# A hybrid decoder layer on one core: the router's logits summed by a picking product, membership written as bf16, and the expert weights and the first splits placed elsewhere

## The chip, the cores and the metric

One Trainium2 chip, one core. The metric is the device time of one execution in microseconds (us); the median of three runs stands for a kernel. Engines in the tables: PE is TensorE, PEld its weight loads, DVE VectorE, ACT ScalarE, POOL GpSimd, SP SyncE (here it issues nearly all DMAs).

## The reference

A layer for 512 tokens of 2048 channels. A mixer (causal pooling and a gated DeltaNet side by side) is added to the residual h; then comes the part that the change touches, a mixture of experts with two-level routing; then a gated per-layer embedding and a final norm.

```python
logits_grp = xf @ w_rg + b_rg                    # 4 groups
gi = argmax(logits_grp); p_sel = softmax(logits_grp)[gi]
logits_exp = (xf @ w_re + b_re).reshape(t, 4, 8)
le = logits_exp[gi]                              # the 8 experts of the chosen group
top_vals, top_idx = lax.top_k(le, 2)
weights = p_sel[:, None] * softmax(top_vals)
...                                              # tokens sorted by expert, in blocks
hmid = silu(xb @ w_gate[e]) * (xb @ w_up[e])     # 2048 -> 512
acc[idx] += (hmid @ w_down[e]) * wt[:, None]     # 512 -> 2048
```

`xf` is rms_norm(h). 32 experts of 12 MB each are read once.

## The kernel before

Tokens lie on partitions in NT = 4 tiles of 128 (P = 128, T = 512, KD = 16 blocks of 128 channels).

`project_out` makes h column block by column block. For each block of 128 channels it transposes h (`h_transposed`), copies the result to `hT` and multiplies with the router's 36 columns `wr` (4 groups and 32 experts). Even blocks add up in partitions 0 to 35 of the PSUM bank `pl`, odd ones in partitions 64 to 99, so the logits are there in two halves, with tokens along the free axis. The last of these products (L921) is followed by the router.

`router` first computes rstd on DVE. Then `L` (named lgT in the rows), which GpSimd had set to zero, takes the two halves of `pl` by two ACT copies (L945); four PE transposes (L947) turn it so that tokens lie on partitions; an ACT copy (L949) brings the bank to SBUF as `l2`; DVE adds the two halves (L960), multiplies by rstd (L961) and adds the bias (L962). `first_max` (L967 to L973) picks the best group (`og`) and then, twice, the best expert (`o1`, `o2`) with tiny DVE operations, each of which reads what the one before wrote. The membership M (L988) is copied to bf16 as `Mb` (L992); ten small products with `Mb` (L995) count the tokens in front, and `rank` (L998) is the place of each token with its expert. The rest of `router` makes the weights of the two chosen experts (`dg`, `gth`, `den`, `psel`, `dm`, `td`, `w`, `wj`, and `aux` in the end), with two tanh on ACT in it.

`spots` makes the 0/1 matrices `G` from `rank` (L1131): eight of 128x128 for the first two units, one per unit and token tile, then larger ones. `gather` multiplies h with `G` (L1161, L1162) to collect the tokens of a unit, 16 channel blocks, two at a time. Each channel block of h, read with a stride of four elements, is first split into a high part `ghi` (ACT, L96) and a low part `glo` (DVE, L97), two buffers each; `L` has the first `ghi` buffer and `l2` the first `glo` buffer, so they are in the same rings. The first two splits, of blocks 0 and 1, may run before the ranks are known.

After that PE multiplies with the expert weights (L1181 up, L1243 down). The weights come in 1 MB transfers through a ring of 16 tiles (`fill_stream`, L1112): SyncE issues the next transfer when PE has used up a tile, and for experts 8 to 31 it reads the expert's number from the table that `order_experts` makes during the first unit.

The order of the instructions of PE is that of the code from `experts` on; on the other engines, and in the router, a scheduler sets it. `behind(ins)` lets what stands in its body be issued only after the given instructions.

Of the kernel before, what the change touches and what calls it, by code (L numbers as in the profile page):

```python
# [9 lines left out]
F32 = mybir.dt.float32  # L10
# [4 lines left out]
OP = mybir.AluOpType  # L15
AX = mybir.AxisListType

P = 128
T = 512
NT = T // P  # L20
# [44 lines left out]
class Layer:  # L65
# [28 lines left out]

    def split(self, hi, lo, src):
        i = self.nc.scalar.copy(hi, src)  # L96
        return i, self.nc.vector.tensor_tensor(lo, src, hi.bitcast(F32), op=OP.subtract)  # L97

# [27 lines left out]
    def constants(self):  # L126
        nc, c, tmp = self.nc, self.consts, self.px
# [3 lines left out]
        nc.gpsimd.iota(pi, pattern=[[0, 1]], base=0, channel_multiplier=1)  # L131
        d = self.below
        self.upper = self.p_dc.tile([P, P], F32, name="upper", bufs=1)
        nc.vector.tensor_scalar(self.upper, d, 0.0, None, op0=OP.is_ge)
# [42 lines left out]
        pr = tmp.tile([P, 8], I32, name="c_pr", bufs=1)  # L177
# [755 lines left out]
    def router(self, pp, pm):  # L933
        nc = self.nc
        pl = self.pl
# [3 lines left out]
        rstd = pp.tile([P, NT], F32, name="rs2", bufs=1)  # L939
# [3 lines left out]
        pt = self.bank("dl")  # L943
        for o in (0, 64):
            nc.scalar.copy(L[o:o + 36, :], pl[o:o + 36, :])  # L945
        for t in range(NT):
            nc.tensor.transpose(pt[:, t * P:(t + 1) * P], L[:, t * P:(t + 1) * P], self.ident)  # L947
        l2 = pm.tile([P, NT, 2, 64], F32, name="l2", tag="glo", bufs=2)
        nc.scalar.copy(l2.rearrange("p t i c -> p (t i c)"), pt)  # L949

        def t_(name, *dims):
            return pp.tile([P, NT, *dims], F32, name=name, bufs=1)

        def bc(x, *dims):
            return x.to_broadcast([P, NT, *dims])

        tt, ts, stt = nc.vector.tensor_tensor, nc.vector.tensor_scalar, nc.vector.scalar_tensor_tensor
        red = nc.vector.tensor_reduce
        lg = t_("lg", 36)
        tt(lg, l2[:, :, 0, 0:36], l2[:, :, 1, 0:36], op=OP.add)  # L960
        tt(lg, lg, bc(rstd[:, :, None], 36), op=OP.mult)  # L961
        tt(lg, lg, bc(self.br[:, None, :], 36), op=OP.add)  # L962
# [23 lines left out]
        tt(o12, o1, o2, op=OP.add)  # L986
        M = t_("M", 4, 8)
        tt(M, bc(og[:, :, :, None], 4, 8), bc(o12[:, :, None, :], 4, 8), op=OP.mult)  # L988
        pr = self.bank("mm")
        Mf = M.rearrange("p t g j -> p t (g j)")  # L990
        Mb = self.p_rt.tile([P, NT, N_EXP], BF16, name="Mb", bufs=1)
        nc.vector.tensor_copy(Mb, Mf)  # L992
        for t in range(NT):
# [3 lines left out]
        self.rank = self.p_rt.tile([P, NT, N_EXP], F32, name="rank", bufs=1)  # L997
        stt(self.rank, pr[:, 0:128].rearrange("p (t e) -> p t e", t=NT), 1.0, Mf, op0=OP.add, op1=OP.mult)  # L998
        self.dump("rank", self.rank)
        dg = t_("dg", 4)  # L1000
        tt(dg, lg[:, :, 0:4], bc(gm, 4), op=OP.subtract)
# [24 lines left out]
        nc.vector.tensor_copy(self.aux[:, :, :, 0], bc(rstd[:, :, None], 4))  # L1026
        self.Mb = Mb

# [107 lines left out]

    def gather(self, pp, G, c0, homes):

# [5 lines left out]
        def parts(k):  # L1144
            hi = pp.tile([P, NT, P], F32R, name="ghi", bufs=2)
            lo = pp.tile([P, NT, P], F32R, name="glo", bufs=2)
            self.split(hi, lo, hs[:, :, k // 4, k % 4, :])
            return hi, lo
# [120 lines left out]
    def experts(self, pp):  # L1269
# [13 lines left out]
        def gathered(*us, spot=None, **kw):  # L1283
            if spot:
                spots(spot, *us, **kw)
            for u in us:
                xe[u] = self.p_xe.tile([P, KD, P], F32, name="xe", tag=f"xe{u % 4}", bufs=1)
            yield from self.gather(pp, *G[us[0]], [xe[u] for u in us])

# [504 lines left out]
```

## Time and profile before

| | |
|---|---|
| median of 3 runs | 2546.78 us (2546.51 to 2548.41) |
| profiled execution | 2548.15 us |
| its span in the trace | 2546.4 us |
| PE busy | 2411.1 us (95% of the span) |
| DVE busy | 1063.4 us (42%) |
| ACT busy | 719.8 us (28%) |
| POOL busy | 83.6 us (3%) |
| DMA | 554.13 MB, mean 218 GB/s |

Times in the rows count from the start of the span. Work outside the span takes 2548.15 - 2546.4 = 1.75 us of the profiled execution. A busy share over the whole span is a mean over stages with different limits: the mixer before 1336 us, the router from 1342 to 1356 us, the experts until 2340 us, the last gate and norm after that.

### The profile page before, as it was taken

To read this page: it belongs to the slowest core of one execution; us is meant where nothing else is said; L and a number is where in the kernel's file an instruction comes from. 1 tells how busy PE (TensorE), PEld (TensorE's weight loads), DVE (VectorE), ACT (ScalarE), POOL (GpSimd) and SP (SyncE) were. 2 spreads that over 40 slices of the span, in tenths; PEclk is the share of its full clock that TensorE was granted. 3 is DMA by queue.
4 is the path that set the end of the run, shared out by engine and by line. 5 is a ranking of instruction groups with operands and counts; after the bars stand their busy time and mean duration, and the time that the engine had idled before them with its cause. 6 is when DMAs were issued, how large, how long until landed. Compare 5 with 4: busy or idle time off the path is not lost. (4 is left out here: it accounts for less than half of the span.)

```text
span 2546.4 us, 30523 instructions
## 1 busy us (share of the span) xinstructions
PE 2411.1 (95%) x11926; PEld 1652.8 (65%) x11926; DVE 1063.4 (42%) x1963; ACT 719.8 (28%) x1323; POOL 83.6 (3%) x92
## 2 busy tenths in 40 slices
PE   7999999999999999999998978999989989987998
PEld 6788888888888888877774523533533433353888
DVE  6475757665422232334445412422423312324435
ACT  5233332423322222224445401400311300114323
POOL 1001011100000000000000000000000000000002
PEclk9999999999999999999998999999999999999999
DMA  5232222233233233247226799999999999998322
GB/s 158 76 88 67 76 72 81 67 97 124 91 99 99 92 99 98 93 155 275 90 88 235 290 386 421 420 421 421 420 421 421 420 380 421 419 419 304 116 83 100
DMA packets 201047, 554.13 MB, mean 218 GB/s; under 512 B 30377, under 2 KB 127042, under 8 KB 152130
## 3 DMA queue, kind: packets, MB, share of 16 engines
q1 hardware_dynamic: 197682, 543.61, 56.2%
q10 hardware_dynamic: 2640, 4.33, 0.5%
q0 software_dynamic: 576, 4.19, 0.4%
q8 instruction: 95, 1.56, 0.3%
q14 instruction: 54, 0.44, 0.0%
HBM read 545.01 MB, written 7.08 MB: 217 GB/s over the span
## 5 line engine op out<-in xcount | busy, mean ns | idle before, releaser
L1181 PE MATMUL ps_mm<-wm,xe 128*64 128x512 f32 (+1 forms) x2048 | 437.9, 607 | 46.5 <-DMA wm<-in_w_up_dram 28.6
L101 PE MATMUL ps_mm<-n1h,whi 128*128 128x512 f32 x1120 | 450.3, 402 | 0.9 <-ACT whi L96 0.9
L103 PE MATMUL ps_mm<-n1h,wlo 128*128 128x512 f32 x1120 | 437.3, 391 | 1.5 <-DVE wlo L97 1.4
L102 PE MATMUL ps_mm<-n1l,whi 128*128 128x512 f32 x1120 | 437.1, 390 | 0.0
L97 DVE TENSOR_TENSOR wlo<-raw,whi 128x1024 fp32r<-128x1024 f32 x206 | 254.5, 1235 | 408.9 <-ACT whi L96 401.1
L96 ACT CAST whi<-raw 128x1024 fp32r<-128x1024 f32 x206 | 216.3, 1050 | 545.1 <-PE ps_mm L102 544.2
L1181 PEld LDWEIGHTS ps_mm<-wm,xe 128*64 128x64 f32 (+1 forms) x2048 | 123.6, 128 | 322.7 <-issue 211.1
L1267 DVE TENSOR_TENSOR h<-h,ps_dl 128x512 f32<-128x512 f32 x208 | 130.2, 682 | 387.6 <-PE ps_dl L1265 387.6
L103 PEld LDWEIGHTS ps_mm<-n1h,wlo 128*128 128x128 f32 x1120 | 210.0, 188 | 47.2 <-DVE wlo L97 2.4
L101 PEld LDWEIGHTS ps_mm<-n1h,whi 128*128 128x128 f32 x1120 | 210.8, 188 | 40.3 <-ACT whi L96 1.3
L102 PEld LDWEIGHTS ps_mm<-n1l,whi 128*128 128x128 f32 x1120 | 210.9, 188 | 38.5
L1243 PE MATMUL ps_mm<-wm,hmT 128*64 128x512 f32 (+1 forms) x896 | 192.1, 610 | 16.7 <-DMA wm<-in_w_down_dram 7.4
L97 DVE TENSOR_TENSOR glo<-h,ghi 128x512 fp32r<-128x512 f32 x80 | 88.7, 1120 | 126.6 <-ACT ghi L96 126.2
L1243 PEld LDWEIGHTS ps_mm<-wm,hmT 128*64 128x64 f32 (+1 forms) x896 | 55.1, 131 | 123.1 <-issue 99.2
L96 ACT CAST ghi<-h 128x512 fp32r<-128x512 f32 x80 | 90.2, 1146 | 137.4 <-PE ps_dl L1161 97.4
L1161 PE MATMUL ps_dl<-G,ghi 128*128 128x384 f32 (+1 forms) x320 | 101.9, 332 | 1.0 <-DVE G L1131 1.0
L103 PE MATMUL ps_mm<-whi,ml 128*128 128x512 f32 x256 | 100.7, 393 | 2.1 <-DVE ml L97 2.1
L101 PE MATMUL ps_mm<-whi,mh 128*128 128x512 f32 x256 | 100.8, 394 | 0.0
L102 PE MATMUL ps_mm<-wlo,mh 128*128 128x512 f32 x256 | 100.7, 394 | 0.0
L1162 PE MATMUL ps_dl<-G,glo 128*128 128x384 f32 (+1 forms) x320 | 98.1, 320 | 1.0 <-DVE glo L97 1.0
L1227 ACT ACTIVATE yhi<-ps_mm,sc 128x512 fp32r<-128x512 f32 x52 | 35.7, 690 | 205.9 <-PE ps_dl L1264 113.6
L1228 DVE SCALAR_TENSOR_TENSOR ylo<-ps_mm,sc,yhi 128x512 fp32r<-128x512 f32 x52 | 39.0, 751 | 118.7 <-ACT yhi L1227 116.6
(417 smaller groups left out, 3292.3 us busy)
## 6 DMA issues: line engine op xcount, KB each, us to landing
wm<-in_w_gate_dram SPq DMA_DIRECT2D x128, 1024.0 KB, 18.9
wm<-in_w_up_dram SPq DMA_DIRECT2D x128, 1024.0 KB, 17.8
wm<-in_w_down_dram SPq DMA_DIRECT2D x128, 1024.0 KB, 19.8
raw<-in_w_in_dram SPq DMA_DIRECT2D x144, 512.0 KB, 3.5
raw<-in_w_out_dram SPq DMA_DIRECT2D x32, 512.0 KB, 3.6
wm<-in_w_ple_gate_dram SPq DMA_DIRECT2D x16, 1024.0 KB, 5.1
raw<-in_w_up_dn_dram SPq DMA_DIRECT2D x16, 512.0 KB, 3.5
raw<-in_w_up_pool_dram SPq DMA_DIRECT2D x16, 512.0 KB, 3.4
```

What stands on the lines that cost most here:

```text
L96: i = self.nc.scalar.copy(hi, src)
L97: return i, self.nc.vector.tensor_tensor(lo, src, hi.bitcast(F32), op=OP.subtract)
L101: mm(ps, whi, xhi, start=start, stop=False)
L102: mm(ps, whi, xlo, start=False, stop=False)
L103: mm(ps, wlo, xhi, start=False, stop=stop)
L1161: nc.tensor.matmul(p, hi[:, t, :], G[:, t, c0:c0 + n], start=t == 0, stop=False)
L1162: nc.tensor.matmul(p, lo[:, t, :], G[:, t, c0:c0 + n], start=False, stop=t == NT - 1)
L1181: nc.tensor.matmul(ps[w * i:w * i + w, :], xe[:, k, w * i:w * i + w], ws[i][:, j, :], start=k == 0, stop=k == KD - 1)
L1227: nc.scalar.activation(yh, ps, AF.Copy, scale=sc[:, 2:3])
L1228: nc.vector.scalar_tensor_tensor(yl, ps, sc[:, 2:3], yh.bitcast(F32), op0=OP.mult, op1=OP.subtract)
L1243: nc.tensor.matmul(out[cb][r, :], hT[:, k, r], ws[i][:, cb * T:(cb + 1) * T], start=k == 0, stop=k == 3)
L1267: nc.vector.tensor_tensor(d, d, pc, op=OP.add)
```

## The change

The router is written anew in five places, and the first two splits of `gather` change engine:

1. The second half of the logits is copied to `L` by DVE, not by ACT.
2. The four transposes become four products with `pick`, a 128x36 matrix with ones where the row is the column or the column plus 64. They transpose and add both halves at once, into 36 columns per token tile. The copy to `l2` and the addition go; the multiplication by rstd reads PSUM.
3. M and its copy become one multiplication that writes `Mb` as bf16; `rank` reads `Mb`.
4. What makes the experts' weights moves into a function `shares`, behind the membership.
5. The low parts of blocks 0 and 1 of the first gather are computed by GpSimd.

```diff
-    def split(self, hi, lo, src):
+    def split(self, hi, lo, src, eng=None):
         i = self.nc.scalar.copy(hi, src)
-        return i, self.nc.vector.tensor_tensor(lo, src, hi.bitcast(F32), op=OP.subtract)
+        return i, (eng or self.nc.vector).tensor_tensor(lo, src, hi.bitcast(F32), op=OP.subtract)
...
+        self.pick = c.tile([P, 36], F32, name="pick")
+        nc.vector.scalar_tensor_tensor(self.pick, d[:, 0:36], -64.0, self.ident[:, 0:36], op0=OP.is_equal, op1=OP.add)
...
         pt = self.bank("dl")
-        for o in (0, 64):
-            nc.scalar.copy(L[o:o + 36, :], pl[o:o + 36, :])
+        nc.scalar.copy(L[0:36, :], pl[0:36, :])
+        nc.vector.tensor_copy(L[64:100, :], pl[64:100, :])
         for t in range(NT):
-            nc.tensor.transpose(pt[:, t * P:(t + 1) * P], L[:, t * P:(t + 1) * P], self.ident)
-        l2 = pm.tile([P, NT, 2, 64], F32, name="l2", tag="glo", bufs=2)
-        nc.scalar.copy(l2.rearrange("p t i c -> p (t i c)"), pt)
+            nc.tensor.matmul(pt[:, t * 36:(t + 1) * 36], L[:, t * P:(t + 1) * P], self.pick, start=True, stop=True)
+        l = pt[:, 0:NT * 36].rearrange("p (t c) -> p t c", t=NT)
...
-        tt(lg, l2[:, :, 0, 0:36], l2[:, :, 1, 0:36], op=OP.add)
-        tt(lg, lg, bc(rstd[:, :, None], 36), op=OP.mult)
+        tt(lg, l, bc(rstd[:, :, None], 36), op=OP.mult)
         tt(lg, lg, bc(self.br[:, None, :], 36), op=OP.add)
...
-        M = t_("M", 4, 8)
-        tt(M, bc(og[:, :, :, None], 4, 8), bc(o12[:, :, None, :], 4, 8), op=OP.mult)
         pr = self.bank("mm")
-        Mf = M.rearrange("p t g j -> p t (g j)")
         Mb = self.p_rt.tile([P, NT, N_EXP], BF16, name="Mb", bufs=1)
-        nc.vector.tensor_copy(Mb, Mf)
+        member = tt(Mb.rearrange("p t (g j) -> p t g j", j=8), bc(og[:, :, :, None], 4, 8),
+                    bc(o12[:, :, None, :], 4, 8), op=OP.mult)
...
-        stt(self.rank, pr[:, 0:128].rearrange("p (t e) -> p t e", t=NT), 1.0, Mf, op0=OP.add, op1=OP.mult)
+        stt(self.rank, pr[:, 0:128].rearrange("p (t e) -> p t e", t=NT), 1.0, Mb, op0=OP.add, op1=OP.mult)
         self.dump("rank", self.rank)
+        self.Mb = Mb
+        with self.behind((member,)):
+            self.shares(t_, bc, rstd, lg, gm, og, m1, m2, o1, o2)
+
+    def shares(self, t_, bc, rstd, lg, gm, og, m1, m2, o1, o2):
...
         dg = t_("dg", 4)
         tt(dg, lg[:, :, 0:4], bc(gm, 4), op=OP.subtract)
...
-    def gather(self, pp, G, c0, homes):
+    def gather(self, pp, G, c0, homes, first=False):
...
-            self.split(hi, lo, hs[:, :, k // 4, k % 4, :])
+            self.split(hi, lo, hs[:, :, k // 4, k % 4, :], nc.gpsimd if first and k < 2 else nc.vector)
...
-            yield from self.gather(pp, *G[us[0]], [xe[u] for u in us])
+            yield from self.gather(pp, *G[us[0]], [xe[u] for u in us], first=us[0] == 0)
```

Two lines are added above the router, so that a line of before stands two to eight lines further down in the kernel after it (L945 becomes L946 and L947, L1131 becomes L1137).

VectorE at the entry of the router, before. `rs` is rstd, `aux` and `glo` are as above, `lg` are the logits, `gm` their maximum over the groups; what stands in brackets is the engine whose signal the instruction waits for.

```order
L1026 COPY aux<-rs_10308 128x16 [waits DVE_49]
L97 TENSOR_TENSOR glo<-h,ghi 128x512
L960 TENSOR_TENSOR lg<-l_10330 128x144 [waits Activation_49]
L961 TENSOR_TENSOR lg<-lg,rs_10308 128x144 [waits DVE_49]
L97 TENSOR_TENSOR glo<-h,ghi 128x512 [waits Activation_49]
L962 TENSOR_TENSOR lg<-lg,br 128x144 [waits DVE_49]
L967 TENSOR_REDUCE gm<-lg 128x4 [waits DVE_49]
```

And after the change:

```order
L89 SCALAR_TENSOR_TENSOR rs_10310<-rsq_b_10312,rsq_j_10311 128x4 [waits DVE_49]
L947 COPY lgT<-ps_dl 36x512 [waits Activation_49]
L961 TENSOR_TENSOR lg<-ps_dl,rs_10310 128x144 [waits DVE_49,PE_49]
L962 TENSOR_TENSOR lg<-lg,br 128x144 [waits DVE_49]
L967 TENSOR_REDUCE gm<-lg 128x4 [waits DVE_49]
L969 TENSOR_TENSOR ge<-lg,gm 128x16 [waits DVE_49]
```

Both splits and the addition have left this place, and the copy to lgT has come to it; it waits for a signal of ScalarE, which in the row of its queue below is its copy of the other half.

ScalarE from there on, after the change:

```order
L946 COPY lgT<-ps_dl 36x512 [waits PE_49,Pool_49]
L96 CAST ghi<-h 128x512 [waits DVE_49,PE_49]
L1010 ACTIVATE gth<-dg 128x16 [waits DVE_49]
L1021 ACTIVATE td<-dm 128x4 [waits DVE_49]
L96 CAST ghi<-h 128x512 [waits PE_49,Pool_49] x2
```

The copies to the second half and to `l2` are gone. The split that follows waits for PE, since its buffer is the one that `L` had; the two tanh (`gth`, `td`) stand behind it, as before.

GpSimd after the change, behind its zeroing of `L`:

```order
L944 MEMSET lgT 128x512 [waits DVE_49]
L1393 IOTA ei 128x32
L97 TENSOR_TENSOR glo<-h,ghi 128x512 [waits DMAHW3_49,DMAHW1_49,DMAHW6_49,DMAHW0_49,Activation_49]
L97 TENSOR_TENSOR glo<-h,ghi 128x512 [waits Activation_49]
L1356 TENSOR_LOAD n_over [waits DVE_49]
```

The two subtractions with `glo` are new in this queue; before, its MEMSET and IOTA were followed at once by the load of `n_over`.

VectorE from the membership to the matrices `G`, before:

```order
L988 TENSOR_TENSOR M<-ge,o_10366 128x128 [waits DVE_49]
L1022 TENSOR_TENSOR wj<-wj 128x4x8 [waits DVE_49]
L992 CAST Mb<-M 128x128 [waits DVE_49]
L1024 TENSOR_TENSOR aux<-ge,wj 128x16x8 [waits DVE_49]
L998 SCALAR_TENSOR_TENSOR rank<-ps_mm,M 128x128 [waits PE_49]
L1131 TENSOR_TENSOR G_10420<-slot,rank 128x128 [waits DVE_49]
L1131 TENSOR_TENSOR G_10420<-slot,rank 128x128 x7
L1131 TENSOR_TENSOR G_10903<-slot,rank 128x4x128 x2
```

And after:

```order
L989 TENSOR_TENSOR Mb<-ge,o_10365 128x128 [waits DVE_49]
L1008 TENSOR_TENSOR dg<-lg,gm 128x16
L1019 TENSOR_TENSOR dm<-am,bm 128x4
L1033 COPY aux<-rs_10310 128x16
L1012 TENSOR_SCALAR den<-gth 128x16 [waits Activation_49]
L1023 TENSOR_SCALAR w_10397<-td 128x4 [waits Activation_49]
L1024 TENSOR_SCALAR w_10397<-td 128x4
L1013 RECIPROCAL den<-den 128x16 [waits DVE_49]
L996 SCALAR_TENSOR_TENSOR rank<-ps_mm,Mb 128x128 [waits PE_49]
L1014 SCALAR_TENSOR_TENSOR den<-gth,den 128x16 [waits DVE_49]
L1137 TENSOR_TENSOR G_10417<-slot,rank 128x128 [waits DVE_49]
L1016 TENSOR_REDUCE psel<-den 128x4 [waits DVE_49]
```

The operations of the weights, which stood between those of the selection, now stand behind the membership: seven of them between `Mb` and `rank`, of which two wait for a tanh of ScalarE, and then one or two behind each of the first six `G`.

## Rows read from the trace of the kernel before

**Rows 1.** Busy time by stage, from the end of the router to the end of the expert weights. Columns: the stretch and its length in us; for each engine the busy us and the number of instructions; PEclk, the granted TensorE clock as a share of full speed; the mean busy share of the 16 DMA engines; GB/s.

```profile
1348.50:1363.00 14.50, 7.18 (x42) 6.65 (x41) 11.31 (x50) 4.80 (x9) 0.00 (x0) 0.54 0.01 4
1363.00:1400.00 37.00, 37.00 (x207) 19.26 (x208) 16.51 (x14) 22.22 (x42) 0.00 (x0) 1.00 0.82 312
...
1485.00:2340.00 855.00, 777.89 (x3861) 337.00 (x3859) 245.32 (x387) 160.27 (x303) 0.00 (x0) 0.98 1.00 414
```

**Rows 2.** What the queue on SyncE that issues the weight transfers waited for between 1330 and 1480 us. Columns: who waited, for whom, us in total, times, longest us.

```profile
SPq L1112 <- PE ps_mm L1181: 75.6, 14, 21.8
...
SPq L1049 <- DVE nb L1426: 9.3, 1, 9.3
```

**Rows 3.** Timeline of the router's entry: from the copies of the two halves of the logits to the addition of the bias. Columns: start in us, duration in us, engine, line, operation, out<-in, count, and in brackets the idle time before it with what ended it.

```profile
1344.58 1.17 ACT L945 COPY lgT<-ps_dl 36x512 f32<-36x512 f32 x2 [1.90 <-PE ps_dl L921]
1345.85 0.63 PE L947 MATMUL ps_dl<-ident,lgT 128*128 128x128 f32 x4 [1.36 <-issue]
1346.51 0.59 ACT L949 COPY l<-ps_dl 128x512 f32<-128x512 f32 x1 [0.76 <-PE ps_dl L947]
1347.00 1.10 ACT L96 CAST ghi<-h 128x512 fp32r<-128x512 f32 x1
1347.13 0.31 DVE L960 TENSOR_TENSOR lg<-l 128x144 f32<-128x144 f32 x1 [1.52 <-ACT l L949]
1347.48 0.31 DVE L961 TENSOR_TENSOR lg<-lg,rs 128x144 f32<-128x144 f32 x1
1348.13 1.06 DVE L97 TENSOR_TENSOR glo<-h,ghi 128x512 fp32r<-128x512 f32 x1 [0.35 <-ACT ghi L96]
1349.11 0.30 DVE L962 TENSOR_TENSOR lg<-lg,br 128x144 f32<-128x144 f32 x1
```

**Rows 4.** Timeline of the chain of small operations on VectorE, with those of the expert weights between them. Columns as in rows 3.

```profile
1349.74 0.17 DVE L1001 TENSOR_TENSOR dg<-lg,gm 128x16 f32<-128x16 f32 x1
1349.86 0.17 DVE L970 TENSOR_TENSOR ge<-ge,prio 128x16 f32<-128x16 f32 x1
1349.94 0.21 ACT L1003 ACTIVATE gth<-dg 128x16 f32<-128x16 f32 x1 [1.84 <-DVE dg L1001]
1350.19 0.17 DVE L1005 TENSOR_SCALAR den<-gth 128x16 f32<-128x16 f32 x1
1350.27 0.17 DVE L973 TENSOR_TENSOR ge<-ge,gq 128x16 f32<-128x16 f32 x1
1350.40 0.25 DVE L1006 RECIPROCAL den<-den 128x16 f32<-128x16 f32 x1
1350.57 0.29 DVE L978 TENSOR_TENSOR le<-lg,ge 128x128 f32<-128x128 f32 x1
...
1353.69 0.19 DVE L986 TENSOR_TENSOR o<-ae,be 128x32 f32<-128x32 f32 x1
...
1354.01 0.28 DVE L988 TENSOR_TENSOR M<-ge,o 128x128 f32<-128x128 f32 x1
...
1354.33 0.23 DVE L992 CAST Mb<-M 128x128 bf16<-128x128 f32 x1
```

**Rows 5.** Timeline from the ranks to the first gather products. Columns as in rows 3.

```profile
1354.61 0.18 PE L995 MATMUL ps_mm<-Mb,before 128*128 128x32 bf16 x1 [8.13 <-DVE Mb L992]
...
1355.07 0.29 DVE L998 SCALAR_TENSOR_TENSOR rank<-ps_mm,M 128x128 f32<-128x128 f32 x1 [0.32 <-PE ps_mm L995]
1355.40 0.90 DVE L1131 TENSOR_TENSOR G<-slot,rank 128x128 fp32r<-128x128 f32 x4
1356.04 0.55 PE L1161 MATMUL ps_dl<-G,ghi 128*128 128x256 f32 x1 [1.00 <-DVE G L1131]
...
1357.46 0.41 PE L1161 MATMUL ps_dl<-G,ghi 128*128 128x256 f32 x1
```

**Rows 6.** Prices read elsewhere. First two rows of a timeline at an expert unit (columns as in rows 3): four products of a 128x128 stationary tile with 9 columns, and four transposes. Then instructions by line: count, duration in ns as minimum/median/maximum, first and last start, shapes.

```profile
1404.55 1.06 PE L1193 MATMUL ps_dl<-aux,G 128*128 128x9 f32 x8
1405.46 0.64 PE L1195 MATMUL ps_dl<-ident,G 128*128 128x128 f32 x4
...
L917 DVE COPY hT<-ps_dl x8: 684/691/693, 1195.4 to 1342.7; 128x512 f32<-128x512 f32 x8
...
L97 DVE TENSOR_TENSOR glo<-h,ghi x80: 1057/1108/1797, 1344.6 to 1999.5; 128x512 fp32r<-128x512 f32 x80
L97 DVE TENSOR_TENSOR ml<-m,mh x64: 684/692/694, 1145.3 to 1330.9; 128x512 fp32r<-128x512 f32 x64
```

**Rows 7.** Timelines of GpSimd and of VectorE at the first chunk of the delta rule, where both work at once. Columns as in rows 3.

```profile
142.76 0.16 DVE L668 TENSOR_TENSOR s<-rk 128x4 f32<-128x4 f32 x1
142.86 1.30 POOL L687 TENSOR_TENSOR bd<-B,diag 128x512 f32<-128x512 f32 x1 [56.98 <-DVE B L684]
142.96 1.22 DVE L669 TENSOR_TENSOR s<-s,beta 128x4 f32<-128x4 f32 x1
...
148.93 1.28 POOL L713 TENSOR_TENSOR E<-E,upper 128x512 f32<-128x512 f32 x1
149.01 1.05 DVE L689 TENSOR_REDUCE bc<-bd 128x64 f32<-128x512 f32 x1 [0.80 <-POOL bd L687]
```

**Rows 8.** GpSimd's elementwise operations on 128x512: by line, with duration in ns as minimum/median/maximum, and by shape, with count | busy us, mean ns | idle before.

```profile
L636 POOL TENSOR_TENSOR gm<-upper,ghi x8: 1040/1050/1712, 81.1 to 481.0; 128x512 fp32r<-128x512 f32 x8
...
L687 POOL TENSOR_TENSOR bd<-B,diag 128x512 f32<-128x512 f32 x8 | 10.3, 1286 | 109.7 <-DVE B L684 80.5 <-DVE s L668 29.2
```

More of the change, by code (lines that the diff above doesn't have):

```diff
@@ L997, in router @@
         self.rank = self.p_rt.tile([P, NT, N_EXP], F32, name="rank", bufs=1)
-        stt(self.rank, pr[:, 0:128].rearrange("p (t e) -> p t e", t=NT), 1.0, Mf, op0=OP.add, op1=OP.mult)
+        stt(self.rank, pr[:, 0:128].rearrange("p (t e) -> p t e", t=NT), 1.0, Mb, op0=OP.add, op1=OP.mult)
         self.dump("rank", self.rank)
+        self.Mb = Mb
+        with self.behind((member,)):
+            self.shares(t_, bc, rstd, lg, gm, og, m1, m2, o1, o2)
+    def shares(self, t_, bc, rstd, lg, gm, og, m1, m2, o1, o2):
+        nc = self.nc
+        tt, ts, stt = nc.vector.tensor_tensor, nc.vector.tensor_scalar, nc.vector.scalar_tensor_tensor
+        red = nc.vector.tensor_reduce
         dg = t_("dg", 4)
@@ L1026, in router @@
         nc.vector.tensor_copy(self.aux[:, :, :, 0], bc(rstd[:, :, None], 4))
-        self.Mb = Mb
     def units(self):
```

## The prediction, made before the changed kernel was run

> **What bounds the kernel now.** I read the busy time by stage first, then the waits of the queue that issues the weights, then the timeline of the router, instruction by instruction. The reader is to see three things.
>
> First, the longest stage, 1485 to 2340 us, is bound by transfers: DMA share 1.00 at 414 GB/s, while PE works 777.89 of 855 us [rows 1]. Nothing in the router makes these 855 us shorter; it can only make them begin sooner. Second, they can begin sooner: between 1348.5 and 1363 us the DMA share is 0.01, since the ring is full, and from 1363 to 1400 PE is busy 37.00 of 37.00 us [rows 1]. The queue that issues the weights waited 75.6 us in 14 waits for PE's up products and 9.3 us for the table of experts, which is itself made behind the first unit [rows 2]. So what the router saves before the first gather product should move all that follows, nearly one for one. Third, in the router PE does nothing for 8.13 us before the rank products [rows 5]; the path runs over ACT and DVE, one small operation after the other.
>
> The path in rows: ACT begins its copies at 1344.58, DVE begins to add the halves at 1347.13 and the bias at 1349.11 [rows 3], M at 1354.01 [rows 4], rank at 1355.07, PE the first gather product at 1356.04 [rows 5]: 11.46 us.
>
> **The change part by part.** Gains are positive; all times are on that path.
>
> *Two engines copy.* DVE's copy waits for ScalarE alone, yet it needs the last router product of PE. Only ACT's copy of the other half has waited for that, so the signal must be that copy's: the two run one after the other, not side by side. Before, they end at 1344.58 + 1.17 = 1345.75 [rows 3]. After: 0.58 for ACT, 0.03 from engine to engine (PE's end 1346.48 to ACT's 1346.51 [rows 3]), and 0.69 for DVE by its copies of 512 elements from PSUM [rows 6]: 1345.88. **-0.13**; were they side by side, 1345.27 and +0.48.
>
> *Picking products.* A transpose is one pass, a product of f32 with f32 two: four transposes show 4 instructions, four products 8, with 0.64 against 1.06 us [rows 6]. **-0.42.** Nine columns there, 36 here; bounds 0 (no dearer) and -0.8 (twice that difference). PE begins 0.10 behind the copies as before, at 1345.98, and ends at 1345.98 + 0.63 + 0.42 = 1347.03.
>
> *The copy to `l2` and the addition.* From PE's end at 1346.48 to DVE at 1347.13 there are 0.65 us [rows 3]; one passage of 0.03 stays: **+0.62**. The addition takes 1347.48 - 1347.13: **+0.35**. Reading PSUM instead costs nothing visible: rank, from PSUM, takes 0.29 [rows 5], M, from SBUF, 0.28 [rows 4].
>
> *The second split leaves DVE.* It sits between the multiplication by rstd and the bias: 1349.11 - 1347.48 = 1.63 us, where the step before took 0.35 [rows 3]: **+1.28**. The first split fills a wait of DVE before 1347.13; moving it gains nothing.
>
> *The weights leave the chain.* Most hide in the gaps between dependent operations: with `dg` and `den` among them the two steps from L970 to L973 take 1350.27 - 1349.86 = 0.41. Only where a reciprocal stands between (1350.57 - 1350.27 = 0.30) and ahead of M, where two `wj` do (1354.01 - 1353.69 = 0.32), is it more than some 0.21 [rows 4]: **+0.19**.
>
> *Where the second split goes.* On GpSimd it meets DVE's chain. Rows show what follows: while POOL ran 142.86 to 144.16, a DVE operation on 128x4 with two SBUF inputs took 1.22 us instead of 0.16 and ended 0.02 behind POOL; a reduction beside the next POOL operation kept its 1.05 [rows 7]. After the change, the multiplication by rstd starts at 1347.03 + 0.03 = 1347.06, the bias at 1347.41. ACT may split `ghi` of block 1 only when the products have released `L`, so 1347.06 to 1348.16 (1.10 [rows 3]); POOL begins then, or behind L970, which starts 0.75 after the bias [rows 4] at 1348.16 and ends at 1348.33. L973, with two SBUF inputs, is due 1.16 after the bias, at 1348.57, and L978 at 1348.77 (1.46, less the reciprocal's 0.10). If POOL takes d, L973 ends 0.02 after 1348.33 + d and L978 starts 0.03 later. For d, contiguous operations show 1.05 and 1.29 [rows 8]; but h is read with stride four, which takes DVE from 0.692 to 1.108 us [rows 6], 1.60 times. I take 1.05 x 1.60 = 1.68, nearest in kind: L978 starts at 1350.06. **-1.29**; with d = 1.05 it is -0.66, with no lock 0.
>
> The Trainium skill (GPSIMD Engine Reference, section 4.1, Engine selection) holds an elementwise operation with two inputs on GpSimd to be about 2 times slower than on VectorE and advises against it. This trace has 1.05 against 0.692, 1.5 times; the page's factor on the 1.06 of the split would be an estimated d of 2.12, and the sum 1.50 - 1.73 = -0.2 us.
>
> *Membership.* The cast saves 0.32, but rank now stands behind two operations that wait for tanh. From the start of M to rank it was 1.06. After, without that wait: 0.28 for M, 0.05 to PE, 0.46 to rank, 0.79. With it: `dg` starts 0.20 after M (as an operation behind a 128x128 one does), `den` 0.45 behind `dg` (1350.19 - 1349.74 [rows 4]), the second tanh ends some 0.2 later, two `w` and a reciprocal follow at 0.1 to 0.15 each: about 1.15. **-0.09**; bounds +0.27 and -0.4. Behind rank wait all `G` and so PE.
>
> *Between the `G`.* Before, `G` starts every 0.20 us (four in 0.90, the last 0.29 long), a pair of them is there every 0.4, and PE takes (1357.46 - 1356.04) / 3 = 0.47 per pair [rows 5], so it waits for the first pair alone. After, `psel` costs the first pair 0.1, and by the fourth pair seven operations of about 0.1 and `aux` make 0.8 against PE's slack of some 0.4 there, counted from the later start. **-0.3**; bounds -0.1 and -0.5. PE waits for the low parts too, but POOL has these by 1350.
>
> Sum without the lock: -0.13 - 0.42 + 0.62 + 0.35 + 1.28 + 0.19 - 0.09 - 0.3 = 1.50. With it: 1.50 - 1.29 = **0.2 us**. The added `pick` is one operation of VectorE of some 0.2 us among the constants, off the path. The profiled execution of 2548.15 becomes 2547.9; it lay 1.4 above the median of 2546.78, which becomes **2546.5** with rounding.
>
> **The rivals.**
>
> *The lock doesn't bite.* POOL could start so that it meets reductions only, or hold DVE for less than its length. For it: L972, a reduction, lies in that stretch. Against: rows 7, and ten operations of the chain within 2 us. Gain 1.5, with side-by-side copies 2.1: 2544.7 to 2545.3.
>
> *The split on GpSimd is long.* It decides from d = 1.91, where 1348.33 + d puts L978 1.50 late. At twice the 1.06 that VectorE takes for this split [rows 3] the loss is 0.2; at 3.0 us it is 1.1: 2547.0 to 2547.9. For it: the stride, and that GpSimd's operations are never shorter than 1.04 here. Against: 1.68 is already a stretched price. This is the case slower than before. By the Trainium skill's page above it is the one to expect.
>
> *The gain does not arrive.* The transfers could absorb it, if their stage began at another signal: 2546.8. Against: rows 2.
>
> *The clock.* PE's mean granted clock is 0.54 from 1348.5 to 1363, where it is busy 7.18 us [rows 1], most of that at 1.2 GHz. If a shorter idle kept it at 2.4 GHz, at most 3.3 us more would go, less where the splits bound the gather: 2542 to 2544. Against: PE still idles some 6 us.
>
> **How the numbers follow.** Forecast (lock of 0.7 to 1.5): 0.50. No lock: 0.22. Long split: 0.15. No arrival: 0.08. Clock: 0.05. The runs of before lie within 1.9 us, and 0.2%, 5.1 us, is about what a measurement can tell from no change. No sum of the cases reaches that, save the clock with no lock and parallel copies (5.4 at most), so faster 0.03, same 0.95, slower 0.02. The range goes from no lock with parallel copies and some noise, 2543.9, to the loss of 1.1 with a little noise, 2548.2.
>
> **What would show it.** In the changed trace: DVE's copy of lgT begins where ACT's ends; the products take about 1.05 us; a two-input operation of the chain, L973 or its neighbour, takes 1 us or more and ends with POOL's second split; `rank` starts 1.0 to 1.2 us behind `Mb`; the first gather product starts some 11 us after ACT's copy. I am wrong if the chain runs through beside POOL, if the split is far from 1.7 us, or if the stage of transfers starts by another amount than the first gather product does.

## The result, and the profile after

The changed kernel takes 2560.91 us (median of 5 runs, 2559.20 to 2564.45) against 2547.79 us (5 runs of the kernel before, 2546.51 to 2548.41): ratio 1.0057, 95% interval 1.0046 to 1.0067. It is slower by some 13 us, where 0.2 us less was forecast and no case reached a loss of more than 1.1 us. The profiled execution of the changed kernel has a span of 2557.2 us, the one of before 2546.4 us.

The router does what the prediction said, nearly row by row. Timeline of the changed kernel from the copies of the logits to the first gather products (start, duration, engine, line, operation; it answers to [rows 3 to 5]):

```profile
1357.03 0.58 ACT L946 COPY lgT<-ps_dl 36x512 f32<-36x512 f32 x1 [1.90 <-PE ps_dl L923]
1357.65 0.69 DVE L947 COPY lgT<-ps_dl 36x512 f32<-36x512 f32 x1 [0.76 <-ACT lgT L946]
1358.39 1.08 PE L949 MATMUL ps_dl<-pick,lgT 128*128 128x36 f32 x8 [1.45 <-DVE lgT L947]
...
1359.51 0.31 DVE L961 TENSOR_TENSOR lg<-ps_dl,rs 128x144 f32<-128x144 f32 x1 [1.17 <-PE ps_dl L949]
1359.86 0.31 DVE L962 TENSOR_TENSOR lg<-lg,br 128x144 f32<-128x144 f32 x1
...
1360.69 1.51 POOL L97 TENSOR_TENSOR glo<-h,ghi 128x512 fp32r<-128x512 f32 x1 [6.76 <-ACT ghi L96]
...
1361.02 1.21 DVE L973 TENSOR_TENSOR ge<-ge,gq 128x16 f32<-128x16 f32 x1
...
1362.26 0.38 DVE L978 TENSOR_TENSOR le<-lg,ge 128x128 f32<-128x128 f32 x1
...
1365.68 0.29 DVE L989 TENSOR_TENSOR Mb<-ge,o 128x128 bf16<-128x128 f32 x1
...
1366.75 0.23 DVE L996 SCALAR_TENSOR_TENSOR rank<-ps_mm,Mb 128x128 f32<-128x128 f32 x1
...
1367.72 0.55 PE L1167 MATMUL ps_dl<-G,ghi 128*128 128x256 f32 x1 [1.27 <-DVE psel L1017]
```

But ScalarE's copy of `lgT`, the first act of the router, starts at 1357.03 where it started at 1344.58 [rows 3]: **12.45 us are lost before any changed operation on the path has run**. The rest follows with that delay. The stage between the gather and the transfers, and what the queue of transfers waits for, are as they were [rows 1, 2]. First busy time by stage (columns as in [rows 1]), then the waits of SyncE's queue (who waited, for whom, us in total, times, longest us):

```profile
1361.00:1375.10 14.10, 6.87 (x43) 5.93 (x42) 11.27 (x45) 4.63 (x10) 1.20 (x1) 0.64 0.01 4
1375.10:1412.00 36.90, 36.90 (x207) 19.22 (x208) 15.20 (x14) 21.66 (x41) 0.00 (x0) 1.00 0.83 313
```

```profile
SPq L1118 <- PE ps_mm L1187: 74.8, 14, 21.5
...
SPq L1055 <- DVE nb L1432: 9.3, 1, 9.3
```

So where do the 12.45 us come from? Matched row by row, the changed kernel falls behind in the mixer: by 0.5 us at 84 us, 3.3 at 620, 3.8 at 660 and 14.0 at 1132, evenly over this last stretch. Some 1.6 us of it (14.0 - 12.45) are made good at the head of the output projection, where some eight products run at the lower granted clock in the trace of before and none in this one; see below. From 660 to 1140 us PE is busy all the time in both. What differs is how many products it gets through. One stretch of the mixer before (us, then busy us and number of instructions of PE, PEld, DVE, ACT, POOL, granted clock, DMA share, GB/s), and two products in its timeline that are 12 apart:

```profile
660.00:1140.00 480.00, 480.00 (x2119) 397.44 (x2119) 136.02 (x133) 108.20 (x120) 0.00 (x0) 1.00 0.32 101
```

```profile
699.94 0.39 PE L101 MATMUL ps_mm<-n1h,whi 128*128 128x512 f32 x1
...
702.66 0.39 PE L101 MATMUL ps_mm<-n1h,whi 128*128 128x512 f32 x1
```

The same of the changed kernel:

```profile
660.00:1140.00 480.00, 480.00 (x2075) 389.20 (x2074) 134.26 (x130) 105.03 (x116) 0.00 (x0) 1.00 0.31 95
```

```profile
704.69 0.39 PE L101 MATMUL ps_mm<-n1h,whi 128*128 128x512 f32 x1
...
707.49 0.39 PE L101 MATMUL ps_mm<-n1h,whi 128*128 128x512 f32 x1
```

2119 against 2075 products in 480 us is 226.5 against 231.3 ns for one; 2119 products thus cost 10.2 us more, what is lost between 660 and 1132 us (14.0 - 3.8). Between neighbours the step is 2.72 / 12 = 0.2267 us before and 2.80 / 12 = 0.2333 after. The mean over the stretch lies below 0.2333 because it also holds products that are as fast as before. The granted clock is 1.00 in both, the instructions are the same, and PE has no idle time. A busy share can't show this: PE reads 480.00 of 480.00 either way.

What does the change alter there? The built programs say it: `pick` (144 B per partition, rounded up to 160) is a tile of the constants, at the left end of SBUF, and every left-side tile opened after it stands 160 B higher. The tiles of the right side stay. A product's stationary operand is the one that PEld loads, its moving operand the other one. Byte addresses per partition of the tiles that the mixer's, the output projection's and the tail's products read, modulo 512 in brackets:

```
                              before          after
whi  (mixer, stationary)      31456 (224)     31616 (384)
n1h0 (mixer, moving)         163808 (480)    163808 (480)
mh   (output projection)      82912 (480)     83072 (128)
whi  (tail, moving)           51936 (224)     52096 (384)
xh   (tail, stationary)      104384 (448)    104384 (448)
```

Call the stationary operand's address less the moving one's, modulo 512, the distance of a product. It goes from 256 to 416 in the mixer; in the output projection both operands move and it stays 256, and there the step stays at 226.9 ns in both traces. (The mixer has some products of this kind too: `yd`, `yh` and `yl` lie on the left like the weights, and keep 256.) In the tail it is 224 before and 64 after, and the step is 233.3 ns in both. That is the theory to test: **a shifted tile, not the router, made the kernel slower.** The rival is that the loss belongs to the changed operations in a way that the rows don't show.

### The profile page after: what moved, and what is told of

It is laid out like the page before. It is cut to its first block, busy times and chain, and to the rows that moved or that the text cites. A ratio compares the mean times of both kernels' runs of the same rounds, so it can differ in the third digit from the quotient of the medians.

```text
span 2557.2 us, 30532 instructions
## 1 busy us (share of the span) xinstructions
PE 2426.1 (95%) x11930; PEld 1648.7 (64%) x11930; DVE 1062.3 (42%) x1961; ACT 717.7 (28%) x1321; POOL 86.6 (3%) x94
## 5 line engine op out<-in xcount | busy, mean ns | idle before, releaser
L101 PE MATMUL ps_mm<-n1h,whi 128*128 128x512 f32 x1120 | 454.9, 406 | 0.9 <-ACT whi L96 0.9
L103 PE MATMUL ps_mm<-n1h,wlo 128*128 128x512 f32 x1120 | 444.0, 397 | 0.9 <-DVE wlo L97 0.8
L102 PE MATMUL ps_mm<-n1l,whi 128*128 128x512 f32 x1120 | 441.9, 395 | 0.0
L103 PEld LDWEIGHTS ps_mm<-n1h,wlo 128*128 128x128 f32 x1120 | 210.1, 188 | 51.7 <-DVE wlo L97 1.7
L102 PEld LDWEIGHTS ps_mm<-n1l,whi 128*128 128x128 f32 x1120 | 210.9, 188 | 45.2
L101 PEld LDWEIGHTS ps_mm<-n1h,whi 128*128 128x128 f32 x1120 | 210.9, 188 | 45.1 <-ACT whi L96 1.3
L103 PE MATMUL ps_mm<-whi,ml 128*128 128x512 f32 x256 | 100.0, 391 | 2.1 <-DVE ml L97 2.1
L102 PE MATMUL ps_mm<-wlo,mh 128*128 128x512 f32 x256 | 100.2, 392 | 0.0
L101 PE MATMUL ps_mm<-whi,mh 128*128 128x512 f32 x256 | 100.1, 391 | 0.0
```

The costliest lines, as they stand in the source:

```text
L101: mm(ps, whi, xhi, start=start, stop=False)
L102: mm(ps, whi, xlo, start=False, stop=False)
L103: mm(ps, wlo, xhi, start=False, stop=stop)
```

## The experiments

In all of them, steps are those between the starts of neighbouring 128x512 products (222 to 242 ns, some 3,060 in the mixer, some 560 in the tail, averaged from the trace).

**e1: the change without its place in SBUF.** `pick` is made in the router's pool, on the right.

```diff
-        self.pick = c.tile([P, 36], F32, name="pick")
-        nc.vector.scalar_tensor_tensor(self.pick, d[:, 0:36], -64.0, self.ident[:, 0:36], op0=OP.is_equal, op1=OP.add)
+        pick = pp.tile([P, 36], F32, name="pick", bufs=1)
+        nc.vector.tensor_tensor(pick, self.ident[:, 0:36], self.ident[:, 64:100], op=OP.add)
```

> The changed kernel with one thing undone: the 36-column picking matrix is made in the router's own pool (right side of SBUF) from two slices of the identity, so that no tile of the left side stands 160 B higher than in the kernel before. Placement theory (the loss is that the 160 B shift of the weight tiles slows every 128x512 product of the mixer from 226.7 to about 233 ns): the mixer is back at 226.7 ns a product, the copy of lgT starts at 1344.6 us as before, and the router's own gain of 1.1 to 1.6 us (the shift falls from 12.45 us at the router's entry to 11.3 and 10.8 us later) is left: 2546.2 to 2547.0 us against some 2547.8 us, ratio 0.9994 to 0.9998. Rival (the loss belongs to the router's rewritten operations or to the split on GpSimd): 2559 to 2561 us, like the changed kernel.

Measured: 2548.81 us (11 runs, 2546.82 to 2550.46) against 2548.34 (27 runs, 2546.88 to 2550.49), ratio 1.0002, interval 0.9993 to 1.0011. The 13 us are gone; the mixer's rate is that of before:

```profile
660.00:1140.00 480.00, 480.00 (x2119) 397.57 (x2119) 135.78 (x133) 108.41 (x120) 0.00 (x0) 1.00 0.33 101
```

The forecast 1.1 to 1.6 us of gain didn't show in the time. It is taken up in "why" below.

**e2: the place without the change.** A pad of 160 B below the mixer's weight tiles in the kernel before, freed with them.

```diff
+        p_pad, s_pad = self.open("pad", "left")
+        pad = p_pad.tile([P, 40], F32, name="pad", bufs=1)
+        self.nc.vector.memset(pad, 0.0)
         self.p_w, s_w = self.open("wstream", "left")
```

> The kernel before with a pad of 160 B per partition below the mixer's weight tiles, freed with them; nothing of the change. Placement theory: n1h and n1l products spaced by 233 ns, router's entry some 12.5 us later (1357 us), time 2559.5 to 2560.7 us, ratio 1.0046 to 1.0051. Rival (the changed code itself costs it): 2547 to 2548.5 us, spacing 226.7 ns.

Measured: 2561.57 us (5 runs, 2560.16 to 2564.25), ratio 1.0054, interval 1.0040 to 1.0068: the whole loss, with none of the change. The same stretch, and the router's entry in the timeline:

```profile
660.00:1140.00 480.00, 480.00 (x2075) 389.23 (x2074) 134.19 (x130) 105.00 (x116) 0.00 (x0) 1.00 0.32 95
```

```profile
1357.09 1.17 ACT L945 COPY lgT<-ps_dl 36x512 f32<-36x512 f32 x2 [1.90 <-PE ps_dl L921]
```

12.51 us late, and 2075 products again. The rival falls.

**e3: both operands moved.** The changed kernel, with 352 B ahead of `n1h` and `n1l` on the right.

```diff
+        p_pad, s_pad = self.open("pad", "right")
+        pad = p_pad.tile([P, 88], F32, name="pad", bufs=1)
+        self.nc.gpsimd.memset(pad, 0.0)
         self.p_n1, s_n1 = self.open("n1", "right")
```

> The changed kernel with a pad of 352 B above it on the right side, so that n1h and n1l lie 352 B lower (128 instead of 480 modulo 512) and the weights stay where the change put them (384 modulo 512): the distance modulo 512 between the two operands is 256 again, as before. If the distance counts: mixer products at 226.7 ns, 2546.2 to 2547.2 us. If the absolute place of the weights counts (the shift off the place they had): 233 ns and 2559 to 2561 us.

Measured: 2546.56 us (10 runs, 2543.86 to 2548.10), ratio 0.9990, interval 0.9981 to 1.0000. The weights stand where the change put them and the products are fast:

```profile
660.00:1140.00 480.00, 480.00 (x2119) 397.45 (x2118) 136.12 (x133) 108.06 (x120) 0.00 (x0) 1.00 0.33 101
```

The distance counts, not the place of either operand.

**e4: the same on the tail,** which stood at 224 before. A small tile, `ms3`, is moved to the pool of the tail's weights, ahead of them, and widened to 480 B, on top of e1.

```diff
-        m = pp.tile([P, NT], F32, name="ms3", bufs=1)
+        m = self.p_w.tile([P, 120], F32, name="ms3", bufs=1)[:, 0:NT]
```

> The kernel of e1 with the tail's weight tiles 480 B higher, so that moving operand (192 modulo 512) and stationary operand (448) stand 256 apart there as well; before they stand 224 apart and the tail's products are spaced by 233.3 ns. If the distance of 256 is what makes a product fast: the tail's 576 products of 128x512 come at 226.7 ns, which is 576 x 6.6 ns = 3.8 us less than e1, and up to 5 us with the narrower products: 2541.5 to 2543.5 us. If not: like e1, 2546 to 2547 us.

Measured: 2545.89 us (11 runs, 2543.80 to 2549.08), ratio 0.9992, interval 0.9983 to 1.0001. That is above the 2541.5 to 2543.5 expected, which started from an e1 of 2546 to 2547 us. The tail's step is 226.7 ns instead of 233.3. In a stretch of it, first e1, then e4:

```profile
2400.00:2480.00 80.00, 80.00 (x344) 64.28 (x343) 32.25 (x30) 24.38 (x38) 12.57 (x8) 1.00 0.28 92
```

```profile
2400.00:2480.00 80.00, 80.00 (x355) 66.26 (x354) 32.15 (x29) 24.48 (x37) 12.62 (x8) 1.00 0.28 94
```

Of the 3.8 us expected, 3.45 are there between 2367 and 2489 us; at the end 1 us of it is gone, since the last products, of 256 columns, step by 120.0 ns instead of 116.7 (383 of them). The medians of e1 and e4 differ by 2.9 us.

**e5 to e8: which distances are fast?** e1 with a constant widened, so that the left side stands 256, 128, 64 or 32 B higher (for 256):

```diff
-        self.before_b = c.tile([P, P], BF16, name="before")
+        wide = c.tile([P, P + 128], BF16, name="before")
+        self.before_b = wide[:, 0:P]
```

> The kernel of e1 with all left-side tiles 256 B higher (a constant widened by 256 B). Distance of the stationary operand's address from the moving one's, modulo 512: mixer 0 instead of 256, tail 480 instead of 224; project_out stays at 256 since both its operands move. If only 256 is fast: mixer products at about 233 ns, some 2560 us. If every multiple of 256 is fast: mixer at 226.7 ns, 2546 to 2550 us; tail at 233.3 ns either way.

> As e5 with 128 B: distances mixer 384, tail 96. If only 256 (or multiples of 256) is fast: mixer at about 233 ns, some 2560 us, tail 233.3 ns. If every multiple of 128 is fast: mixer 226.7 ns, 2546 to 2550 us.

> As e5 with 64 B: distances mixer 320, tail 160. If only 256 is fast: mixer at about 233 ns, some 2560 us. If multiples of 64 are fast: mixer 226.7 ns, 2546 to 2550 us; tail 233.3 ns either way, since 160 is no multiple of 64.

> As e5 with 32 B, the smallest step of a tile: distances mixer 288, tail 192. If only 256 is fast: mixer at about 233 ns, some 2560 us, tail 233.3 ns. If the tail's 192 is fast where its 224 was not (multiples of 64): tail 226.7 ns, some 3.8 us less there.

Measured, one run each beside a run of before at 2552.37 us: 2550.43, 2560.90, 2561.11 and 2559.28 us. The stretch of the mixer in e5, e6, e7 and e8:

```profile
660.00:1140.00 480.00, 480.00 (x2119) 397.61 (x2118) 135.40 (x133) 108.80 (x120) 0.00 (x0) 1.00 0.33 101
```

```profile
660.00:1140.00 480.00, 480.00 (x2077) 389.68 (x2076) 133.84 (x130) 104.89 (x116) 0.00 (x0) 1.00 0.32 96
```

```profile
660.00:1140.00 480.00, 480.00 (x2077) 388.52 (x2076) 134.23 (x130) 105.04 (x116) 0.00 (x0) 1.00 0.32 96
```

```profile
660.00:1140.00 480.00, 480.00 (x2077) 389.67 (x2076) 133.01 (x130) 105.11 (x115) 0.00 (x0) 1.00 0.32 96
```

All that was measured, by distance (mean step in ns, m for mixer, o for output projection, t for tail; the means in the mixer hold a few waits, 227.7 is 226.7 without them):

| distance | step | run |
|---|---|---|
| 256 | m 227.7, o 226.9, t 226.7 | before, e1, e3; all but e11; e4 |
| 0 | m 227.7 | e5 |
| 192 | t 228.9 | e8 |
| 224, 480 | t 233.3 | before, e5 |
| 64, 96, 160 | t 233.3, 234.3, 233.3 | after, e6, e7 |
| 288, 320, 384, 416 | m 233.1, 233.2, 232.6, 233.3 | e8, e7, e6, after |

0 and 256 are fast, the others cost 6 to 7 ns a product, save 192, which costs about 2. The steps of a slow product can be uneven (after: 231, 232 and 237 ns by turns; e7: 233 and 234), those of a fast one are 226 or 227. Only 256 was tried in all three stages; 0, 288, 320, 384 and 416 were tried in the mixer alone, and 64, 96, 160, 192, 224 and 480 in the tail alone, where the weights are the moving operand. The runs don't tell a period of 512 B from one of 256 B.

**e9: both splits back on VectorE,** on top of e1: the price of the lock and of the split that it replaces.

```diff
-            self.split(hi, lo, hs[:, :, k // 4, k % 4, :], nc.gpsimd if first and k < 2 else nc.vector)
+            self.split(hi, lo, hs[:, :, k // 4, k % 4, :], nc.vector)
```

> The kernel of e1 with the first two splits back on VectorE, so that nothing runs on GpSimd beside the router's chain. By the prediction's terms the lock (-1.29) goes and the second split's 1.28 comes back: L973 takes 0.17 us instead of 1.21, a split of 1.06 us stands in the chain instead, and from ACT's copy of lgT to the first gather product it is 10.6 to 10.8 us, against 10.70 in e1 and 11.46 before. Rival (the lock isn't what held L973, or the split fits a gap of the chain): 9.5 to 9.9 us. The time says nothing at this size; the kernel's end should be within 1.5 us of e1.

Measured: 2547.51 us in one run, against 2545.62 for the kernel before (15 runs); its span of 2545.7 us is within 1.5 us of e1's 2546.5, as expected. Its rows, and the same two ends of the chain in e1:

```profile
1344.24 0.58 ACT L946 COPY lgT<-ps_dl 36x512 f32<-36x512 f32 x1 [2.51 <-PE ps_dl L921]
...
1347.06 0.31 DVE L962 TENSOR_TENSOR lg<-lg,br 128x144 f32<-128x144 f32 x1
...
1347.85 1.06 DVE L97 TENSOR_TENSOR glo<-h,ghi 128x512 fp32r<-128x512 f32 x1 [0.48 <-ACT ghi L96]
...
1348.82 0.16 DVE L967 TENSOR_REDUCE gm<-lg 128x4 f32<-128x16 f32 x1
...
1349.64 0.17 DVE L973 TENSOR_TENSOR ge<-ge,gq 128x16 f32<-128x16 f32 x1
...
1355.31 0.55 PE L1167 MATMUL ps_dl<-G,ghi 128*128 128x256 f32 x1 [1.27 <-DVE psel L1017]
```

```profile
1343.30 0.58 ACT L946 COPY lgT<-ps_dl 36x512 f32<-36x512 f32 x1 [1.90 <-PE ps_dl L921]
...
1354.00 0.55 PE L1167 MATMUL ps_dl<-G,ghi 128*128 128x256 f32 x1 [1.27 <-DVE psel L1017]
```

Without GpSimd L973 takes 0.17 us instead of 1.21: the lock is real. The split now stands in the chain behind the bias, where L967 comes 1.76 us after L962 instead of 0.35, and the first gather product starts 11.07 us after the copy, a little later than the 10.6 to 10.8 expected; in e1 these were 1354.00 - 1343.30 = 10.70. By these two traces the split on GpSimd is worth 0.37 us.

**e10: the tail's 256-column products at the distance that looked best for them,** on top of e4.

```diff
+            o = 0 if w == 512 else 48
-            hi = self.p_w.tile([P, 1024], F32R, name="whi", bufs=4)
+            hi = self.p_w.tile([P, 1152], F32R, name="whi", bufs=4)[:, o:o + 1024]
```

(and `wlo` alike).

> The kernel of e4 with the tail's weight tiles of 256 columns 192 B higher, at a distance of 64 from the tokens (the changed kernel had this distance and 113.4 ns a product of 256 columns; e1 at 224 had 116.7 and e4 at 256 had 119.7). If the distance sets it: 512-column products of the tail 226.7 ns, 256-column products 113.4 ns; against e1 576 x 6.6 + 384 x 3.3 = 3.8 + 1.3 = 5.1 us less, 2543 to 2544 us, ratio to the kernel before 0.9977 to 0.9985. If it does not: like e4, ratio 0.9985 to 0.9998.

Measured: 2542.91 us (11 runs, 2540.86 to 2544.80) against 2545.62 (15 runs), ratio 0.9988, interval 0.9979 to 0.9997: it beats the kernel before (medians), by some 2.7 us, and, by the two ratios (0.9988 and 1.0057), the changed one by some 17. But the reason given for its last step was wrong: the 256-column products step by 117.8 ns, not 113.4, and e3, which has the changed kernel's distance there too, shows 117.8 as well. For them the distance doesn't set the step. What is gained is the 512-column part.

**e11: only one of the two stationary tiles moved.** A pad of 160 B between `whi` and `wlo`, on top of e1.

```diff
         hi = self.p_w.tile([P, 1024], F32R, name="whi", bufs=2)
+        if not hasattr(self, "wpad"):
+            self.wpad = self.p_w.tile([P, 40], F32, name="wpad", bufs=1)
+            nc.gpsimd.memset(self.wpad, 0.0)
         lo = self.p_w.tile([P, 1024], F32R, name="wlo", bufs=2)
```

> The kernel of e1 with a pad of 160 B between whi and wlo, so that of the mixer's stationary tiles only wlo moves: distances to n1h and n1l are 256 for whi and 416 for wlo. (The tiles behind it move too: yd, yh, yl, mh and ml then stand 96 from whi and 256 from wlo.) The mixer repeats three products: L101 streams n1h over whi, L102 streams n1l over whi, L103 streams n1h over wlo. If what costs time is the load of the next product's weights beside the stream of the present one, the step from L102 to L103 (wlo is loaded then) grows from 226.7 to about 233 ns and the other two stay. If it is a product's own weights, the step from L103 to L101 grows and the one from L102 to L103 stays. With yd, yh and mh next to whi at distance 96, two of three of their steps should grow as well; in all some 10 to 13 us more than e1 either way.

Measured: 2567.92 us in one run, against 2547.98: 20 us, more than the 10 to 13 expected.

```profile
660.00:1140.00 480.00, 480.00 (x2068) 387.72 (x2067) 134.54 (x131) 105.52 (x116) 0.00 (x0) 1.00 0.31 95
```

All three steps of the mixer grow: L101 to L102 from 227.5 to 233.8 ns, L102 to L103 from 227.7 to 234.1, L103 to L101 from 227.8 to 232.0. With `wlo` at a bad distance, the step between the two products over `whi`, at the good one, is slow too. Neither account, a product's own weights or the load of the next ones, predicts that. In the output projection the pad moves one of two moving tiles: `whi` stands 416 from `mh` and `ml` (the expectation's 96 counts the other way), `wlo` 256 from `mh`. There the steps from L101 to L102 and from L103 to L101 grow to 233.3 and 234.9 ns, and the one behind L102, which streams `wlo`, only to 228.4. Of the 20 us, 16.2 are lost when the output projection begins (1159.74 against 1143.52 in e1) and 3.8 more when the router does (1363.31 against 1343.30). How the two operands get in each other's way stays open.

## Why the prediction was wrong

**The step that failed** is a sentence beside the sum: "The added `pick` is one operation of VectorE of some 0.2 us among the constants, off the path." As an operation it is off the path. As a tile it is not: e2 has the tile's shift and nothing else and is as slow as the changed kernel, e1 has all else and is not. The prediction counted instructions and waits, and took it that the rest of the program runs as before; a term for the addresses of the mixer's operands was missing: 14.0 us at the end of the mixer, of which 12.45 are left at the router's entry.

A rule of the Trainium skill (SBUF — State Buffer, Who interferes with whom) would have spoken for leaving it out: it gives PE two independent read ports, one for the moving operand and one for the load of weights, and says that PE waits on no one. The measurement doesn't fit that: with the same instructions and the granted clock at 1.00, a product takes 226.7 or 233.3 ns by where its two operands lie to each other (e1, e2, e3). Whether the two reads are what gets in each other's way, no run here shows. The same section has an operation of VectorE with two inputs in SBUF contend with one of GpSimd that reads SBUF; there the trace agrees, 1.21 us for L973 beside GpSimd and 0.17 without (e9).

**The router's terms** held. On the path, from [rows 3 to 5] and the rows of after:

| term | forecast | measured |
|---|---|---|
| two engines copy, one after the other | -0.13 | (1358.34 - 1357.03) - 1.17: -0.14 |
| picking products | -0.42 | 1.08 against 0.63: -0.45 |
| copy to `l2` | +0.62 | 1359.51 - 1359.47 = 0.04 against 0.65: +0.61 |
| addition | +0.35 | +0.35 |
| second split leaves VectorE | +1.28 | L961 to L962 0.35 against 1.63: +1.28 |
| weights leave the chain | +0.19 | bias to M: 5.82 - 1.04 (lock) = 4.78 against 4.90: +0.12 |
| lock | -1.29 | 1.21 against 0.17 for L973: -1.04 |
| M to `rank` | -0.09 | 1366.75 - 1365.68 = 1.07 against 1.06: -0.01 |
| all, to ScalarE's next split of h | 0.2 | 12.45 - 12.26 = 0.19 |

The lock was over-priced by 0.25: GpSimd's split takes 1.51, not 1.68 us, and it starts 0.83 behind the bias, not 0.92. By the Trainium skill (GPSIMD Engine Reference, section 4.1, Engine selection), which the prediction cited, an estimate for the split was 2.12 us, twice VectorE's time. The trace has 1.51 / 1.06 = 1.4 times. What the lock gave back went at the step "between the `G`": the first gather product starts 12.45 - (1367.72 - 1356.04) = 0.77 us better, and 0.19 of it is left at ScalarE's next split, so that step costs 0.58, not 0.3, more than its bound of 0.5. The split, before and after:

```profile
1357.91 1.14 ACT L96 CAST ghi<-h 128x512 fp32r<-128x512 f32 x1 [4.63 <-PE ps_dl L1161]
```

```profile
1370.17 1.15 ACT L96 CAST ghi<-h 128x512 fp32r<-128x512 f32 x1 [3.77 <-PE ps_dl L1167]
```

In e1, which has the old addresses, the same two points give 0.76 and 0.19 (copy at 1343.30, split at 1356.44). One sum of the prediction is off without consequence: in its long-split rival the gain is used up from d = 1.89 on (1350.27 - 1348.33 - 0.05), not 1.91.

**Why not even e1 shows a gain.** In its trace e1 enters the router 1.28 us ahead of before and the tail 1.17 ahead, and ends level. What it is ahead and what it gives back are mostly TensorE's clock. At the head of the tail PE waits for splits and falls to the lower level; from which product on the clock is back differs from trace to trace. Before, then e1:

```profile
2352.00:2358.00 6.00, 2.89 (x10) 2.17 (x10) 5.62 (x8) 5.95 (x12) 0.00 (x0) 0.76 0.06 8
2358.00:2360.00 2.00, 2.00 (x9) 1.63 (x8) 1.93 (x6) 0.00 (x0) 0.00 (x0) 0.87 0.83 287
```

```profile
2352.00:2358.00 6.00, 3.59 (x9) 2.82 (x10) 5.63 (x8) 4.77 (x10) 0.00 (x0) 0.61 0.19 53
2358.00:2360.00 2.00, 2.00 (x6) 1.62 (x5) 1.73 (x10) 0.00 (x0) 0.00 (x0) 0.50 1.07 392
```

In the traces of this case, with and without the change, 5 (before) to 13 (e3) products of the tail step by 0.43 us, the lower level, instead of 0.23 before the clock is back: 0.2 us each, up to 1.6 us between traces. The start of the output projection does the same. Before gets through 15 products at a granted clock of 0.66, e1 through 20 at 1.00:

```profile
1146.00:1151.00 5.00, 4.95 (x15) 3.95 (x16) 3.01 (x4) 0.62 (x1) 0.00 (x0) 0.66 1.05 429
```

```profile
1146.00:1151.00 5.00, 4.62 (x20) 3.85 (x21) 3.35 (x5) 0.62 (x1) 0.00 (x0) 1.00 1.02 421
```

There is one trace for each kernel, so that the traces alone don't tell a difference between kernels from one between executions; but the mean granted clock does differ between executions of one kernel: in the 27 runs of before beside e1 it lies between 0.986 and 0.991. Against that, 0.2 us from the router can't be seen in the time, which the prediction said of any gain of this size; it said nothing of a loss of 13. The 1.1 to 1.6 us that e1's expectation took for the router's own gain were read from the trace of after, and most of them are made elsewhere: the shift of 12.45 us is still 12.05 when the stage of transfers begins, 11.22 at its end, and falls by another 1.2 in the last products of the tail, which step by 113.3 ns in that trace and by 116.7 before.

The times alone leave open whether the router's new form pays. e3 has all of it and fast products in the mixer, and its median is 1.8 us below before; e1 has the same operations in the router and is 0.5 us above. Their traces (2546.3 and 2546.5 us) don't show what parts them. At the first expert product the traces give the router 0.2 to 0.4 us: it starts 18.44 us behind ScalarE's copy before (1363.02), 18.18 in e1 (1361.48) and 18.06 after.

**The chances.** 0.95 for "no difference", against 0.02 for slower, came from rivals that were all in the router or behind it. The right rival, that an added tile moves others, needed no trace to be named: the diff adds a tile to a pool below everything. But no row of the trace of before would have priced it, save the tail's 233.3 against the mixer's 226.7 ns, which stood there for the same shape at the same clock and was not asked about.

## What to carry to other kernels

A tile added to a pool that opens early is a change to every later tile on its side: compare the addresses of the operands of the hottest products before and after, not only the order of instructions. When a whole stage shifts evenly and its engine is busy throughout, compare how many instructions it completes in a fixed stretch; busy shares and waits are blind to it. And where two stages run the same shape at the same clock at different steps, the slower one may have something to give: here some 3 us for a widened tile (e4 against e1).

## What the runs showed of the hardware

For 128x512 products of f32 data in reduced-precision form, each with its own 128x128 weights, the step is 226.7 ns where the two operands' addresses differ by a multiple of 256 B (0 and 256 modulo 512 were tried), and 232.6 to 234.3 ns at nine other distances tried (192: 228.9). Moving either operand changes it, moving both by the same amount doesn't. One stationary tile of two at a bad distance slows all three steps of the pattern (232.0 to 234.1); one moving tile of two slows the steps of its own two products (233.3 and 234.9) and the third only to 228.4 (both e11). Products of 256 columns step by 113 to 120 ns with no order by distance. GpSimd's split of a strided 128x512 tile takes 1.51 us against 1.06 on VectorE, and holds up an operation of VectorE with two inputs in SBUF until it ends (1362.23 against 1362.20).
